# Shared weight tiles for a k pair and more pairs in seven products in a float32 decoder trunk

## The chip, the cores and the metric

The kernel runs on one core of one Trainium2 chip. TensorE does the matrix products, VectorE (DVE in the profile) the elementwise work on two operands, ScalarE (ACT) copies, casts and activation functions, GpSimd (POOL) a few small steps, and SyncE (SP) issues nearly all DMAs. The metric is the time of one execution on the device in microseconds; lower is better. Three runs of the kernel before stand beside one profiled execution.

## The reference

Two pre-norm layers over a stream of 256 positions and 2048 features, all in float32. Layer 0 mixes by sliding-window attention and an mLSTM memory, layer 1 by an attention with forget gates; each is followed by a SwiGLU feed-forward part with 5632 hidden features. The change lies in the feed-forward part and in how weights are loaded:

```python
def swiglu(xn, w_gate, w_up, w_down):
    return (jax.nn.silu(xn @ w_gate) * (xn @ w_up)) @ w_down
...
        h = h + mix.astype(h.dtype)
        h = h + swiglu(rms_norm(h, norm_ffn[layer]), w_gate[layer], w_up[layer], w_down[layer])
    return rms_norm(h, norm_final)
```

## The kernel before

**Three products for one.** A float32 product is made of products on float32r operands. An operand is split in a high part, a rounded copy (ScalarE's cast), and a low part, the difference (VectorE). One product is then three matmuls into the same PSUM bank: high by high, high by low, low by high (`three`, L365 to L368, and the same in `gemm`, L187 to L189). Each is 128x128 weights against 128 x 512 columns. The activations (xh, xl, mh, ml) are split once; the weights come from memory, two k tiles of 512 columns at a time (`load_raw`, tile raw, `CK = 2`), and are split by `split_chunk` into hi (L159, ScalarE) and lo (L160, VectorE). There are six buffers each of hi and lo, four of raw.

**Groups of the feed-forward part.** The 256 positions are two tiles t of 128. `pair_group` (from L373) computes the products of both t with two blocks of 512 columns, `mats`: the same columns of w_gate and w_up, or two neighbouring blocks of w_down. These four results have four PSUM banks (`plain`). It walks over pairs of k tiles in the order of a table of (kind, pair): `ORDER` for gate and up (8 pairs), `DOWN` for the down product (6 or 8 pairs).

- Kind 0, a plain pair: for both matrices a load, a split, and 4 products of three matmuls; 24 matmuls.
- Kind 1, a mixed pair: the 2x2 blocks (two positions tiles, two k tiles, two matrices) are multiplied in seven products, not eight; 21 matmuls. It needs sums of activations (sx, sd; made once by `sums_of`, L222 on) and sums of weight tiles: four VectorE operations of 512 columns into t4 (L404 to L407), split into ht (L261) and lt (L262), two tiles of two k tiles each, besides hi and lo of the first matrix and of one k tile of the second. Four of the seven products go into four further banks (`prods`), which are added up into c when the group's last mixed pair is done (L430 to L434).

The banks swap: the plain banks of a group are the prods banks of the next. Before the change 3 of 8 pairs are mixed in gate/up, 1 of 6 or 2 of 8 in down.

**Order of the groups.** The 11 gate/up groups of a layer are cut in parts (`PARTS`: groups 0 to 2, 3 to 6, 7 to 10). After each part come two down groups over its hidden features; in the last part of layer 1 the second is replaced by two plain `gemm` runs, with `skew` k tiles at their end sorted by t, so that the first t finishes early. After a gate/up group, silu and the product with up are formed on ScalarE and VectorE, and the result is transposed by DMA; the rest of this (`join`) is put into the next group, once its sixth position (or fifth) is reached: copies, a split into mh and ml, and the sums for mixed pairs.

**Who orders the work.** Each engine runs its queue strictly in order. The order in a queue is set when the program is built: a scheduler goes through the operations of all engines by a planned time, so TensorE's matmuls need not stand in the order of the code. A tile of a pool is given out again when all work on the tile that had the buffer is done.

## Time and profile before

| | |
|---|---|
| runs | 2135.94 us median of 3 (2135.59 to 2136.3) |
| profiled execution | span 2134.3 us |
| TensorE | 2118.0 us busy, 9772 matmuls |
| VectorE | 1665.9 us busy, 2116 instructions |
| ScalarE | 1235.5 us busy, 1564 instructions |
| DMA | 418.84 MB, mean 196 GB/s |
| granted clock | 0.998 of full speed |

The feed-forward part of layer 0 lies at about 350 to 1000 us, that of layer 1 at about 1430 to 2134 us; before them are the projections and attention of their layers. In the rows of the trace a line starts with the time from the span's start and the duration, in microseconds; L366 is line 366 of the kernel, and `acc<-lo,xh` says that a matmul writes the tile acc from lo and xh. Groups of rows have a count (x198) and a mean in ns. `<-ACT ht L261` behind a row names what ended an idle time. A matmul row lasts 0.39 us, but the next one starts after 0.23 us, since they are pipelined.

### The profile page before, as it was taken

Reading aid. Unit: us, or ns where it says so; the run is one execution under the profiler, and the core shown is the slowest. Engines: PE = TensorE matmul, PEld = TensorE weight load, DVE = VectorE, ACT = ScalarE, POOL = GpSimd, SP = SyncE. Lnnn points to the kernel's source line nnn. Section 1 sums busy time; section 2 is a strip of 40 time slices with the busy share of each in tenths; the row PEclk is TensorE's granted clock in tenths of the full one; section 3 lists DMA queues with packets and bytes.
Section 4 is the critical chain, followed back from the end, with each engine's and each line's share of the span. In section 5 each row is a group of like instructions: output and inputs, shape, how many; then the busy total and the mean of one; then the engine's idle time right before and its main releaser. Section 6 shows DMA issues by size and latency. Waiting matters only on the chain.

```text
span 2134.3 us, 26801 instructions
## 1 busy us (share of the span) xinstructions
PE 2118.0 (99%) x9772; PEld 1758.6 (82%) x9772; DVE 1665.9 (78%) x2116; ACT 1235.5 (58%) x1564; POOL 40.4 (2%) x61
## 2 busy tenths in 40 slices
PE   8999999999999999999999999999999999999998
PEld 7888888888888888888888888888888888888886
DVE  6665567998899988998745554768998998889984
ACT  6565455665567646666645544556754667556753
POOL 2010000000000000000010000000000000000000
PEclk9999999999999999999999999999999999999999
DMA  8444556666667666776575564655756666656753
GB/s 268 149 151 145 174 183 206 214 210 194 200 205 223 212 206 193 236 210 191 152 236 168 168 178 141 234 185 174 246 187 215 207 207 199 234 188 207 227 198 128
DMA packets 257060, 418.84 MB, mean 196 GB/s; under 512 B 56256, under 2 KB 64544, under 8 KB 256672
## 3 DMA queue, kind: packets, MB, share of 16 engines
q1 hardware_dynamic: 256256, 413.40, 61.1%
q0 software_dynamic: 624, 3.72, 0.5%
q8 instruction: 76, 1.25, 0.2%
q14 instruction: 56, 0.46, 0.1%
q10 hardware_dynamic: 48, 0.02, 0.0%
HBM read 404.48 MB, written 2.11 MB: 191 GB/s over the span
## 4 chain that ended last, share of the span: by engine, by line
PE 98%; ACT 1%; issue 0%; DMA 0%; DVE 0%; POOLq 0%; POOL 0%; DVEq 0%; ACTq 0%
PE acc L367 17%; PE acc L368 17%; PE acc L366 17%; PE acc L187 10%; PE acc L188 10%; PE acc L189 10%; PE prod L368 4%; PE prod L367 4%; PE prod L366 4%; PE pt L239 1%; PE p L290 1%; PE ptm L273 1%; PE po L341 1%; PE pp L333 0%; PE p L283 0%
## 5 line engine op out<-in xcount | busy, mean ns | idle before, releaser
L159 ACT CAST hi<-raw 128x1024 fp32r<-128x1024 f32 (+1 forms) x692 | 705.7, 1033 | 681.2 <-PE acc L368 308.4
L160 DVE TENSOR_TENSOR lo<-raw,hi 128x1024 fp32r<-128x1024 f32 (+1 forms) x692 | 820.4, 1198 | 317.9 <-ACT hi L159 316.3
L367 PE MATMUL acc<-lo,xh 128*128 128x512 f32 x946 | 368.1, 389 | 0.0
L368 PE MATMUL acc<-hi,xl 128*128 128x512 f32 x946 | 366.8, 389 | 0.0
L366 PE MATMUL acc<-hi,xh 128*128 128x512 f32 x946 | 366.4, 389 | 0.0
L187 PE MATMUL acc<-hi,xh 128*128 128x512 f32 (+3 forms) x736 | 276.6, 377 | 0.8 <-ACT hi L159 0.8
L189 PE MATMUL acc<-hi,xl 128*128 128x512 f32 (+3 forms) x736 | 276.6, 376 | 0.0
L188 PE MATMUL acc<-lo,xh 128*128 128x512 f32 (+3 forms) x736 | 276.3, 375 | 0.0
L368 PEld LDWEIGHTS acc<-hi,xl 128*128 128x128 f32 x946 | 177.6, 188 | 36.8
L367 PEld LDWEIGHTS acc<-lo,xh 128*128 128x128 f32 x946 | 177.6, 188 | 36.8
L366 PEld LDWEIGHTS acc<-hi,xh 128*128 128x128 f32 x946 | 177.6, 188 | 36.8
L262 DVE TENSOR_TENSOR lt<-t,ht 128x1024 fp32r<-128x1024 f32 x168 | 199.6, 1216 | 3.6 <-ACT ht L261 3.6
L367 PE MATMUL acc<-lo,mh 128*128 128x512 f32 x514 | 200.3, 390 | 0.0
L366 PE MATMUL acc<-hi,mh 128*128 128x512 f32 x514 | 200.1, 389 | 0.0
L368 PE MATMUL acc<-hi,ml 128*128 128x512 f32 x514 | 198.6, 389 | 0.0
L261 ACT CAST ht<-t 128x1024 fp32r<-128x1024 f32 x168 | 175.0, 1053 | 23.2 <-PE acc L368 13.1
L187 PEld LDWEIGHTS acc<-hi,xh 128*128 128x128 f32 x736 | 138.8, 189 | 24.9 <-ACT hi L159 1.2
L189 PEld LDWEIGHTS acc<-hi,xl 128*128 128x128 f32 x736 | 139.1, 189 | 24.3 <-issue 0.8
L188 PEld LDWEIGHTS acc<-lo,xh 128*128 128x128 f32 x736 | 139.1, 189 | 24.1 <-issue 0.7
L187 PE MATMUL acc<-hi,mh 128*128 128x512 f32 x320 | 125.8, 393 | 1.2 <-ACT mh L261 1.2
L188 PE MATMUL acc<-lo,mh 128*128 128x512 f32 x320 | 125.7, 393 | 0.0
L189 PE MATMUL acc<-hi,ml 128*128 128x512 f32 x320 | 124.0, 390 | 0.0
(306 smaller groups left out, 2768.4 us busy)
## 6 DMA issues: line engine op xcount, KB each, us to landing
raw<-in_w_gate_dram SPq DMA_DIRECT2D x176, 512.0 KB, 4.1
raw<-in_w_up_dram SPq DMA_DIRECT2D x176, 512.0 KB, 4.5
raw<-in_w_down_dram SPq DMA_DIRECT2D x176, 512.0 KB, 4.6
raw<-in_w_in_odd_dram SPq DMA_DIRECT2D x88, 512.0 KB, 3.8
raw<-in_w_in_even_dram SPq DMA_DIRECT2D x64, 512.0 KB, 3.8
raw<-in_w_out_even_dram SPq DMA_DIRECT2D x32, 512.0 KB, 3.5
raw<-in_w_out_odd_dram SPq DMA_DIRECT2D x32, 512.0 KB, 3.9
raw<-in_w_in_odd_dram SPq DMA_DIRECT2D x8, 272.0 KB, 2.9
```

The lines of the kernel that those rows point to most:

```text
L159: latest[0] = nc.scalar.copy(hi[:, :, 0:n], raw[:, :, 0:n])
L160: nc.vector.tensor_tensor(out=lo[:, :, 0:n], in0=raw[:, :, 0:n], in1=hi[:, :, 0:n].bitcast(F32), op=ALU.subtract)
L187: nc.tensor.matmul(o, ah[:, ts], hi, start=(k == 0), stop=False)
L188: nc.tensor.matmul(o, ah[:, ts], lo, start=False, stop=False)
L189: nc.tensor.matmul(o, al[:, ts], hi, start=False, stop=(k == k_all - 1))
L239: nc.tensor.transpose(pt[:, i, t, :], h[:, t, k * P : (k + 1) * P], ident)
L261: nc.scalar.copy(dst_h, src)
L262: nc.vector.tensor_tensor(out=dst_l, in0=src, in1=dst_h.bitcast(F32), op=ALU.subtract)
L273: nc.tensor.transpose(pt[:, i, :], s_, ident)
L366: nc.tensor.matmul(o, ah, hi, start=start, stop=False)
L367: nc.tensor.matmul(o, ah, lo, start=False, stop=False)
L368: nc.tensor.matmul(o, al, hi, start=False, stop=stop)
```

## The change

A weight tile raw now holds four k tiles of 512 columns (`CK = 4`), and there are three of them, shared by everything; hi and lo are as wide, with three buffers each. In the projections and `gemm` a chunk is four k tiles, loaded by two DMAs as large as before. In `pair_group` one raw tile holds a k pair of both matrices (`load_pair`): the second matrix in blocks 0 and 1, the first in 2 and 3. A plain pair is then split by one cast and one difference of 2048 columns. In a mixed pair one split covers three blocks; the four sums are formed by one operation of 1024 columns (its first operand repeated) into td, and two of 512 columns written back into raw; ht and lt are one tile each of four blocks, with one buffer, filled by two splits. Products that need no sums go to TensorE in another order, and the third sum of the activations changes its sign.

The tables have one more mixed pair in the even gate/up groups (positions 1, 3, 5, 6), and in every down group (2 of 6, 3 of 8). The odd gate/up groups keep three, at positions 2, 4 and 6. In the down groups the four adds into h become one, and the last `gemm` sorts its last eight k tiles, not six.

```diff
-CK = 2
+CK = 4
+PK = 2
...
-ORDER = ((0, 0), (0, 1), (1, 2), (0, 4), (1, 3), (0, 5), (1, 6), (0, 7))
+ORDER = (
+    ((0, 0), (1, 1), (0, 2), (1, 3), (0, 4), (1, 5), (1, 6), (0, 7)),
+    ((0, 0), (0, 2), (1, 1), (0, 4), (1, 3), (0, 5), (1, 6), (0, 7)),
+)
 DOWN = {
-    6: ((0, 0), (0, 1), (1, 2), (0, 3), (0, 4), (0, 5)),
-    8: ((0, 0), (0, 1), (0, 3), (1, 2), (0, 4), (1, 5), (0, 6), (0, 7)),
+    6: ((0, 0), (0, 1), (1, 2), (0, 3), (1, 4), (0, 5)),
+    8: ((0, 0), (1, 1), (0, 2), (1, 3), (0, 4), (1, 5), (0, 6), (0, 7)),
 }
...
-    wp = ctx.enter_context(tc.tile_pool(name="wp", bufs=6))
-    wr = ctx.enter_context(tc.tile_pool(name="wr", bufs=4))
+    wp = ctx.enter_context(tc.tile_pool(name="wp", bufs=3))
+    wr = ctx.enter_context(tc.tile_pool(name="wr", bufs=3))
...
+    def load_pair(mats, k0):
+        raw = wr.tile([P, CK, NB], F32, tag="raw", name="raw")
+        for half, (w, c0) in zip((PK, 0), mats):
+            fetch(raw[:, half : half + PK, :], w, k0, c0, NB)
         return raw
...
-        if n < 3:
+        if n < 2:
             ahead.append(load_raw(wi, n * CK, OFF_KS, NB))
...
-            ra, rb = (load_raw(w, k0, c0, NB, fp) for w, c0 in mats)
-            hg, lg = split_chunk(ra, NB)
+            raw = load_pair(mats, k0)
+            hg, lg = split_chunk(raw[:, 1:4, :], NB)
             run_due(todo, pos)
-            t4 = fp.tile([P, 4, NB], F32, tag="t4", name="t4", bufs=1)
-            nc.vector.tensor_tensor(out=t4[:, 0, :], in0=rb[:, 0, :], in1=ra[:, 0, :], op=ALU.subtract)
-            nc.vector.tensor_tensor(out=t4[:, 1, :], in0=rb[:, 1, :], in1=rb[:, 0, :], op=ALU.subtract)
-            nc.vector.tensor_tensor(out=t4[:, 2, :], in0=rb[:, 1, :], in1=t4[:, 0, :], op=ALU.subtract)
-            nc.vector.tensor_tensor(out=t4[:, 3, :], in0=ra[:, 1, :], in1=t4[:, 2, :], op=ALU.subtract)
-            hu = wp.tile([P, CK, NB], F32R, tag="hi", name="hi")
-            lu = wp.tile([P, CK, NB], F32R, tag="lo", name="lo")
-            split_plain(hu[:, 1, :], lu[:, 1, :], rb[:, 1, :])
-            ht, lt = [], []
-            for i in range(2):
-                hs = fp.tile([P, 2, NB], F32R, tag="ht", name="ht")
-                ls = fp.tile([P, 2, NB], F32R, tag="lt", name="lt")
-                split_plain(hs, ls, t4[:, 2 * i : 2 * i + 2, :])
...
+            td = fp.tile([P, 2, NB], F32, tag="td", name="td", bufs=1)
+            nc.vector.tensor_tensor(
+                out=td, in0=raw[:, 0:1, :].broadcast_to([P, 2, NB]), in1=raw[:, 1:3, :], op=ALU.subtract
+            )
+            nc.vector.tensor_tensor(out=raw[:, 0, :], in0=raw[:, 1, :], in1=td[:, 1, :], op=ALU.subtract)
+            nc.vector.tensor_tensor(out=raw[:, 1, :], in0=raw[:, 3, :], in1=raw[:, 0, :], op=ALU.subtract)
+            ht = fp.tile([P, 4, NB], F32R, tag="ht", name="ht", bufs=1)
+            lt = fp.tile([P, 4, NB], F32R, tag="lt", name="lt", bufs=1)
+            split_plain(ht[:, 0:2, :], lt[:, 0:2, :], td)
+            split_plain(ht[:, 2:4, :], lt[:, 2:4, :], raw[:, 0:2, :])
             sh, sl = sums(pair)
...
+            three(plain[0][0], xb[:, t0], lb[:, t0], hg[:, 2, :], lg[:, 2, :], False, False)
+            three(plain[1][0], sh[:, 3, :], sl[:, 3, :], hg[:, 0, :], lg[:, 0, :], False, False)
+            three(prods[0], xa[:, t0], la[:, t0], hg[:, 1, :], lg[:, 1, :], first, last)
+            three(prods[1], sh[:, 0, :], sl[:, 0, :], ht[:, 1, :], lt[:, 1, :], first, last)
+            three(prods[2], sh[:, 2, :], sl[:, 2, :], ht[:, 0, :], lt[:, 0, :], first, last)
+            three(prods[3], sh[:, 1, :], sl[:, 1, :], ht[:, 2, :], lt[:, 2, :], first, last)
+            three(plain[0][1], xb[:, t1], lb[:, t1], ht[:, 3, :], lt[:, 3, :], False, False)
...
-                        gemm(acc, m_of, wd, n * NB, NB, 0, nk, nk, skew=3 if n == 3 else 1)
+                        gemm(acc, m_of, wd, n * NB, NB, 0, nk, nk, skew=2 if n == 3 else 1)
```

More of the change, by code (lines that the diff above doesn't have):

```diff
@@ L42 @@
 MID_DOWN = 5
-RAWS = 4
 PARTS = (0, 3, 7, 11)
@@ L99, in trunk, with fetch, load_raw @@
     nc.scalar.dma_start(gn[0], norm_mix.rearrange("l (k p) -> (l k) p", p=P))
-    def load_raw(w, k0, c0, n, pool=wr):
-        raw = pool.tile([P, CK, NB], F32, tag="raw", name="raw", bufs=4 if pool is wr else RAWS)
-        nc.sync.dma_start(
-            raw[:, :, 0:n], w[k0 * P : (k0 + CK) * P, c0 : c0 + n].rearrange("(k p) n -> p k n", p=P)
-        )
+    def fetch(raw, w, k0, c0, n):
+        m = raw.shape[1]
+        nc.sync.dma_start(raw[:, :, 0:n], w[k0 * P : (k0 + m) * P, c0 : c0 + n].rearrange("(k p) n -> p k n", p=P))
+    def load_raw(w, k0, c0, n):
+        raw = wr.tile([P, CK, NB], F32, tag="raw", name="raw")
+        for half in range(0, CK, PK):
+            fetch(raw[:, half : half + PK, :], w, k0 + half, c0, n)
+        return raw
+    def load_pair(mats, k0):
+        raw = wr.tile([P, CK, NB], F32, tag="raw", name="raw")
+        for half, (w, c0) in zip((PK, 0), mats):
+            fetch(raw[:, half : half + PK, :], w, k0, c0, NB)
         return raw
@@ L248, in split_scaled @@
             pair = 2 * n + half
-            if extra is not None and pair in mixed_of(ORDER):
+            if extra is not None and pair in mixed_of(ORDER[0]):
                 sh, sl, pool = extra
-                j = mixed_of(ORDER).index(pair)
+                j = mixed_of(ORDER[0]).index(pair)
                 def copies(full):
@@ L440, in sums_x @@
         def sums_x(pair):
-            j = mixed_of(ORDER).index(pair)
+            j = mixed_of(ORDER[0]).index(pair)
             return sx[0][:, j, :, :], sx[1][:, j, :, :]
```

54 lines of the change are left out of this document (22 added, 32 removed).

## The prediction

> **What bounds the kernel now.** I read the page first (busy times, slices, the chain that ended last), then what TensorE waited for, then the FFN by windows, one for each group of matmuls.
>
> ```profile
> span 2134.3 us, 26801 instructions
> PE 2118.0 (99%) x9772; PEld 1758.6 (82%) x9772; DVE 1665.9 (78%) x2116; ACT 1235.5 (58%) x1564; POOL 40.4 (2%) x61
> DVE  6665567998899988998745554768998998889984
> PEclk9999999999999999999999999999999999999999
> PE 98%; ACT 1%; issue 0%; DMA 0%; DVE 0%; POOLq 0%; POOL 0%; DVEq 0%; ACTq 0%
> ```
>
> TensorE is busy for 99% at the full clock, and the chain lies on it for 98%. VectorE is the next: 78% overall, but 8s and 9s in the two FFN stretches. Busy time of pipelined matmuls can hide small gaps, so the waits:
>
> ```profile
> PE pg L144 <- DMA gn<-in_norm_mix_dram: 4.1, 1, 4.1
> PE acc L187 <- ACT mh L261: 1.2, 1, 1.2
> PE pt L239 <- DMA h<-in_x_dram: 1.1, 1, 1.1
> PE acc L187 <- ACT hi L159: 0.8, 1, 0.8
> PE pp L333 <- DVE s L325: 0.2, 1, 0.2
> ```
>
> TensorE waits for almost nothing after the first microseconds. Now the second part of the FFN of layer 0: gate/up groups 3, 4, 5, 6 and two down groups (a window, its length, busy time of each engine).
>
> ```profile
> core 0: us, PE busy (x) PEld busy (x) DVE busy (x) ACT busy (x) POOL busy (x), PEclk, DMA share, GB/s
> 540.40:581.88 41.48, 41.48 (x184) 34.36 (x183) 32.18 (x37) 22.41 (x24) 0.00 (x0) 1.00 0.66 213
> 581.88:623.36 41.48, 41.48 (x184) 34.36 (x183) 38.26 (x46) 27.56 (x30) 0.00 (x0) 1.00 0.68 216
> 623.36:664.84 41.48, 41.48 (x184) 34.36 (x183) 39.25 (x50) 28.41 (x31) 0.00 (x0) 1.00 0.68 216
> 664.84:706.32 41.48, 41.48 (x184) 34.36 (x183) 38.59 (x50) 28.30 (x31) 0.00 (x0) 1.00 0.69 213
> 706.32:748.48 42.16, 42.16 (x187) 34.92 (x186) 37.19 (x45) 26.39 (x28) 0.00 (x0) 1.00 0.63 201
> 748.48:790.64 42.16, 42.16 (x187) 34.92 (x186) 36.43 (x44) 20.41 (x21) 0.00 (x0) 1.00 0.62 201
> ```
>
> A gate/up group has 183 matmuls and 41.48 us: 0.2267 us each, without a gap. VectorE has 2.2 to 3.2 us of room in a group that also joins the one before. So fewer matmuls save their full 0.2267 us as long as VectorE and ScalarE deliver in time, and the room there is some 7%.
>
> **The change, part by part.** *Matmuls removed.* A pair of k tiles costs 24 matmuls plainly and 21 in seven products. One more pair is mixed in six of eleven gate/up groups of each layer (0, 2, 4, 6, 8, 10) and in each of six down groups, in layer 1 five: 23 pairs, 69 matmuls, 69 x 0.2267 = **-15.6 us**.
>
> *VectorE's work.* One instruction after the other takes:
>
> ```profile
> 568.83 0.69 DVE L404 TENSOR_TENSOR t<-raw 128x512 f32<-128x512 f32 x1
> 569.44 0.68 DVE L405 TENSOR_TENSOR t<-raw 128x512 f32<-128x512 f32 x1
> 570.04 0.68 DVE L406 TENSOR_TENSOR t<-raw,t 128x512 f32<-128x512 f32 x1
> 570.64 1.22 DVE L160 TENSOR_TENSOR lo<-raw,hi 128x1024 fp32r<-128x1024 f32 x1
> 571.78 0.68 DVE L407 TENSOR_TENSOR t<-raw,t 128x512 f32<-128x512 f32 x1
> ```
>
> From start to start 0.60 us for 512 columns, 1.14 for 1024; 0.54 for each further 512 makes 1.67 for 1536 and 2.21 for 2048. A mixed pair was 3 x 1.14 (lo, two lt) + 5 x 0.60 = 6.42, and becomes 1.67 + 1.14 (td) + 2 x 0.60 + 2 x 1.14 = 6.29. A plain pair goes from 2.28 to 2.21. An even gate/up group (four mixed, four plain) gains 34.0 - 30.66 = 3.3: the windows' 38.26 and 38.59 become 41.6 and 41.9, or 1.4 more where a join now has sums to form (four 128x128 operations and a split). TensorE needs 180 x 0.2267 = 40.8. An odd group loses 0.7 (39.25 becomes 38.5, of 41.48); a down group gains 3.2 and stays under 41.5. Over these six windows VectorE goes from 221.9 to 235 of 247.5: no bound on the whole, but over TensorE in the even groups, where a lead won before must carry it.
>
> *The ht and lt tiles, the term that decides.* Before, ht and lt were two tiles of two columns blocks, released half by half; now they are one tile of four with one buffer. How such a release goes in the profile:
>
> ```profile
> 564.65 0.39 PE L368 MATMUL prod<-ht,sx 128*128 128x512 f32 x1
> 565.12 1.06 ACT L261 CAST ht<-t 128x1024 fp32r<-128x1024 f32 x1
> 566.01 0.39 PE L368 MATMUL acc<-ht,xl 128*128 128x512 f32 x1
> 566.41 2.39 DVE L262 TENSOR_TENSOR lt<-t,ht 128x1024 fp32r<-128x1024 f32 x2
> 566.49 1.05 ACT L261 CAST ht<-t 128x1024 fp32r<-128x1024 f32 x1 [0.30 <-DVE lo L160]
> 573.72 0.39 PE L366 MATMUL prod<-ht,sx 128*128 128x512 f32 x1
> ```
>
> The second product on ht ends its half at 565.04 and ScalarE refills it at 565.12; the last ends at 566.40, and the other half is refilled at 566.49. These halves are used at 573.72: a plain pair and nine matmuls lie between, and hide the split. I compared the order written for TensorE in the changed kernel. After the last matmul that reads a mixed pair's ht comes, before the first that reads the next pair's: in groups 0, 2, 6 and 10 of both layers, where positions 5 and 6 are both mixed, **one** matmul; in group 8 none; in group 4 fifteen; in group 5 and 9 (positions 2 and 4) and in the first down group of the last part (3 and 5) six; elsewhere nine or more.
>
> From the start s of that last matmul: it ends at s + 0.39, ScalarE starts at s + 0.48 as above, a half is copied by s + 1.53, TensorE starts 0.06 later (the start-up rows below: cast ends 8.19, matmul 8.25), at s + 1.59. The second half follows at ScalarE's spacing, some 0.96 (two casts in 2.00 us in the row 573.31, quoted below), so TensorE can use it at s + 2.55.
>
> ```profile
> 573.31 2.00 ACT L159 CAST hi<-raw 128x1024 fp32r<-128x1024 f32 x2
> 576.68 1.05 ACT L261 CAST ht<-t 128x1024 fp32r<-128x1024 f32 x1 [0.30 <-PE acc L368]
> ```
>
> With one matmul between, the first would have started at s + 0.45: 1.14 lost; the third at s + 2.04 waits for the second half: 0.51 more, 1.65. Eight such: 13.2. Group 8, none between, first half only: 1.59 - 0.23 = 1.36, twice: 2.7. Six between: 0.51, six times: 3.1. Sum **+19.0 us**. Bounds: nothing, if the halves are released singly after all; and 1.2 us more in each of the ten (the 1024 lt after the ht, if VectorE comes to it late, as the next group's lo stands before the lt in its queue in groups 8 and 10), 31. I take 19: each link has its row.
>
> The Trainium skill (Perfetto Trace Analysis, Optimization Strategy) says that a gap which repeats on the engine that should be saturated can mean too few buffers for the next tile. No gap repeats in this trace; by that rule this single buffer would make one, and its sum is the one just made.
>
> *The start of the even groups.* Prods of the old group lie in the banks that the new group's plain products want; VectorE must empty them. In group 6 and 10 VectorE has, from the last lt of the old group to the bank of the third product, sd 0.60, td 1.14, lo 1.67, u 0.60, raw 0.60, lt 1.14 and c 0.60: 6.35. TensorE has 20 matmuls in between, 4.53; counted on in the same way from the release before, VectorE's last lt stands 1 us ahead of its need, so 0.8 is lost, and as much again at the lo of the third pair that stands behind. 1.6 in four groups: **+6.2**. Bounds: none, and 3 us in all ten even groups with a mixed pair second after another group, 30. I take the count.
>
> *Start-up.* The first chunk has now four k tiles:
>
> ```profile
> 7.16 1.03 ACT L159 CAST hi<-raw 128x1024 fp32r<-128x1024 f32 x1
> 8.23 1.22 DVE L160 TENSOR_TENSOR lo<-raw,hi 128x1024 fp32r<-128x1024 f32 x1 [0.45 <-ACT hi L159]
> 8.25 1.22 PE L187 MATMUL acc<-hi,xh 128*128 128x512 f32 x2 [0.83 <-ACT hi L159]
> ```
>
> The cast and the difference double, 2.1 us later at most for both, and another 512 KB must land; transposes now go ahead of the first matmul and win some back. Between 0 and 4, taken **+1.5**. The Trainium skill (Perfetto Trace Analysis, Optimizing Scalar/DVE Operations) speaks against larger operations here: where these engines are not saturated but make others wait, breaking them up can help; by it the loss would be nearer the 4.
>
> *At nothing.* The loads and their time to land:
>
> ```profile
> raw<-in_w_gate_dram SPq DMA_DIRECT2D x176, 512.0 KB, 4.1
> raw<-in_w_down_dram SPq DMA_DIRECT2D x176, 512.0 KB, 4.6
> ```
>
> They stay as many and as large; one pair fewer is in flight, but a pair lasts 4.8 us or more on TensorE, as long as a load takes. Chunks of four in the projections and output: TensorE never waits there now, and two more tiles are ready; without that cover 1 us each. Three adds fewer per down group on VectorE, the new sign in the sums, the longer sorted tail (it frees the first half earlier, the last matmul ends the same): 0, within 0.5. ScalarE copies the same columns; its 28 of 41.5 us leave room, its order matters only in the chain above. POOL and its queue are unchanged.
>
> Sum: -15.6 + 19.0 + 6.2 + 1.5 = +11.1. The span becomes 2145.4; the median of the runs, 2135.94, lies 1.6 above the span, so **2147**.
>
> **The rivals.** *One: the cover holds and the matmuls are saved.* If ht is freed by halves or VectorE and ScalarE keep ahead, only start-up and the odd 0.5 remain: -15.6 + 1.5 + 0 to 3 gives 2122 to 2125. For it: no wait of TensorE in the FFN now, 94.9% of VectorE in the stretch. Against: one matmul of cover against a chain of 1.59 us. It decides below some 0.6 us lost at each of the ten places, together with the group starts.
>
> *Two: VectorE becomes the bound of the even groups.* Then each of eight groups with a join lasts VectorE's 41.9 to 43.0 and the 2.2 us that it idles even now: 44.1 to 45.2 against 41.48, +2.6 to +3.7, 21 to 30 us; the ends of the other groups give back 8, start-up takes 1.5: 2150 to 2160. For it: 8s and 9s in the slices, 95% in group 5. Against: much of the idle is a wait for tiles that TensorE frees, and is filled when VectorE is late.
>
> *Three: gains and waits cancel*, within 4 us of before: what happens if the group starts cost nothing and the chain a little less.
>
> **How the numbers follow.** Forecast (2138 to 2155 by itself) 0.45; rival two, or both mechanisms in full up to 2168, 0.25; rival one 0.22; rival three 0.08. A difference under 0.2% (4.3 us) can't be told from none. So faster 0.22, same 0.08, slower 0.70. The range leaves out the lower half of rival one and the upper end of rival two: 2124 to 2163.
>
> **What would show it.** TensorE's matmuls fall by 69. In even groups except 4 there is a gap of 1.1 us or more before the first product on ht of position 6, its releaser ScalarE's ht copy, with a second of 0.5 behind; even groups last 42 to 44.5 us instead of 40.8, down groups about 41.5. If TensorE's waits for ht stay under 5 us in all, the chain was wrong; if the even groups last long with TensorE waiting for lo and lt, VectorE's total was the cause; if start-up moves by over 4, the chunk size.

## The result and the profile after

The changed kernel takes 2271.65 us (median of four runs, 2269.23 to 2274.98) against 2135.99 before: a ratio of 1.0638, 95% interval 1.0623 to 1.0653. It is slower, as forecast, but by 135.7 us and not by 11: the range ended at 2163. The profiled execution has a span of 2267.5 us in a run of 2269.23.

The page of the changed kernel, its busy times, VectorE's slices and the chain that ended last:

```profile
span 2267.5 us, 25185 instructions
PE 2165.9 (96%) x9703; PEld 1753.1 (77%) x9703; DVE 1727.9 (76%) x1766; ACT 1215.0 (54%) x1234; POOL 39.0 (2%) x61
...
DVE  5565567988889898889645555578888988789885
...
PE 45%; DVE 21%; DMA 17%; ACT 8%; issue 5%; SPq 2%; ACTq 0%; DVEq 0%; POOLq 0%; POOL 0%
```

The 69 matmuls are gone (9772 to 9703). VectorE is busy for 62 us more with 350 instructions fewer, about as counted (13 us more in six of the 33 groups that `pair_group` walks); ScalarE is busy for 20 us less. TensorE's busy time grew by 48 us with fewer matmuls, so its 96% do not measure its gaps. What stands out is the chain. It lay on TensorE for 98% and now does for 45%; DMA, which had nothing of it, has 17%, VectorE 21%. TensorE waits for an engine that itself waits, at the far end for a load.

Where it waits is seen one step further up, in what ScalarE waited for (us in all, times, longest). After:

```profile
ACT hi L172 <- DMA raw<-in_w_up_dram: 211.4, 93, 8.6
ACT hi L172 <- DMA raw<-in_w_down_dram: 100.2, 33, 6.0
```

and before, the same two places:

```profile
ACT hi L159 <- DMA raw<-in_w_gate_dram: 14.6, 9, 1.6
ACT hi L159 <- DMA raw<-in_w_down_dram: 13.9, 10, 5.7
```

ScalarE's cast of fresh weights now waits 312 us for loads, eleven times as long. Of the waits that TensorE itself has on record, 91.6 us in all, 41.2 are for these casts, 14.3 for lo and 8.8 for ht. That is less than what was lost; the rest lies inside TensorE's busy time.

By windows, for groups of layer 0 (a window from the first matmul of a group to the next group's; its length, busy time of each engine, clock):

```profile
core 0: us, PE busy (x) PEld busy (x) DVE busy (x) ACT busy (x) POOL busy (x), PEclk, DMA share, GB/s
353.05:400.94 47.89, 44.53 (x191) 35.42 (x190) 37.57 (x45) 26.99 (x32) 0.69 (x1) 0.96 0.46 155
442.71:492.90 50.19, 44.64 (x182) 34.43 (x180) 43.95 (x44) 29.69 (x25) 0.00 (x0) 0.97 0.57 187
747.80:791.99 44.19, 42.08 (x185) 34.20 (x183) 37.57 (x36) 26.95 (x23) 0.00 (x0) 1.00 0.62 199
836.15:877.63 41.48, 41.48 (x184) 34.37 (x183) 36.68 (x31) 19.32 (x15) 0.00 (x0) 1.00 0.57 185
```

Groups 0 and 2 last 47.9 and 50.2 us where their 180 matmuls take 40.8; a down group 44.2 where it should take 41.5; group 7, behind two down groups, runs without a gap. In group 0 VectorE has only 37.6 us of work: it cannot be the whole cause.

One gap read through the engines, at the end of group 10 of layer 0 (rows of ScalarE, SyncE's queue, VectorE and TensorE):

```profile
985.32 1.49 ACT L172 CAST hi<-raw 128x1536 fp32r<-128x1536 f32 x1 [1.07 <-DMA raw<-in_w_up_dram]
...
988.45 5.96 SPq L495 DMA_TRANSPOSE turned<-c  x4
994.51 0.53 SPq L106 DMA_DIRECT2D raw<-in_w_gate_dram  x1
...
999.22 0.69 DVE L421 TENSOR_TENSOR raw<-raw 128x512 f32<-128x512 f32 x1
1005.12 1.22 DVE L275 TENSOR_TENSOR lt<-raw,ht 128x1024 fp32r<-128x1024 f32 x1
...
1004.09 0.88 SPq L106 DMA_DIRECT2D raw<-in_w_down_dram  x2
1009.55 1.90 ACT L172 CAST hi<-raw 128x2048 fp32r<-128x2048 f32 x1 [5.85 <-DMA raw<-in_w_down_dram]
1011.36 1.04 ACT L274 CAST ht<-td 128x1024 fp32r<-128x1024 f32 x1
1011.50 0.50 PE L379 MATMUL acc<-hi,mh 128*128 128x512 f32 x1 [2.78 <-ACT hi L172]
1012.45 0.73 PE L379 MATMUL prod<-ht,sx 128*128 128x512 f32 x2 [0.45 <-ACT ht L274]
...
1014.42 0.63 PE L380 MATMUL acc<-lo,mh 128*128 128x512 f32 x1
1014.85 0.63 PE L381 MATMUL acc<-hi,ml 128*128 128x512 f32 x1
```

The mixed pair that is cast at 985.32 has its last sum at 999.22, but that sum lies in the load tile itself, and the lt made from it ends at 1006.34: the tile is held for 21 us from its cast, 26.6 from the issue of its load at 979.78, and the last 6.4 of them, from the end of the sum at 999.91, for the lt alone. Only three tiles exist. So the next group's first load is not issued before 1004.09, when another tile is freed, and lands at 1009.5; ScalarE stands 5.85 us, with the ht copies of the last mixed pair, whose data are there, behind the waiting cast; and TensorE stops for both. Ahead of the pair of loads at 994.51 four transposes hold SyncE's queue for 5.96 us.

A gap costs more than its own length here. The matmuls at 1014.42 and 1014.85 start 0.43 us apart, not 0.23, and the granted clock is 0.88 from 1003.90 to 1018.50. Over the whole span it is 0.985, which lacks 0.015 x 2267.5 = 34 us of full speed, against 4 before (0.998): by this estimate up to 30 of the 135.7 us are slow matmuls behind gaps.

### The profile page after: what moved, and what is told of

Read it like the earlier page. It is cut to its first block, busy times and chain, and to the rows that moved or that the text cites. A ratio compares the mean times of both kernels' runs of the same rounds, so it can differ in the third digit from the quotient of the medians.

```text
span 2267.5 us, 25185 instructions
## 1 busy us (share of the span) xinstructions
PE 2165.9 (96%) x9703; PEld 1753.1 (77%) x9703; DVE 1727.9 (76%) x1766; ACT 1215.0 (54%) x1234; POOL 39.0 (2%) x61
## 4 chain that ended last, share of the span: by engine, by line
PE 45%; DVE 21%; DMA 17%; ACT 8%; issue 5%; SPq 2%; ACTq 0%; DVEq 0%; POOLq 0%; POOL 0%
DMA raw<-in_w_up_dram 11%; PE acc L202 10%; PE acc L201 10%; PE acc L200 10%; DVE lo L173 10%; DMA raw<-in_w_down_dram 5%; ACT hi L172 5%; PE acc L380 3%; DVE lt L275 3%; PE acc L381 3%; PE acc L379 3%; DVE td L417 2%; ACT ht L274 1%; SPq L495 1%; SPq L106 1%
## 5 line engine op out<-in xcount | busy, mean ns | idle before, releaser
L173 DVE TENSOR_TENSOR lo<-raw,hi 128x2048 fp32r<-128x2048 f32 (+4 forms) x388 | 814.4, 2101 | 342.8 <-ACT hi L172 341.9
L172 ACT CAST hi<-raw 128x2048 fp32r<-128x2048 f32 (+4 forms) x388 | 680.7, 1757 | 691.7 <-PE acc L202 221.4
L379 PE MATMUL acc<-hi,mh 128*128 128x512 f32 x437 | 165.2, 402 | 27.3 <-ACT hi L172 19.4
L380 PE MATMUL acc<-lo,mh 128*128 128x512 f32 x437 | 175.1, 401 | 6.9 <-DVE lo L173 6.9
L381 PE MATMUL acc<-hi,ml 128*128 128x512 f32 x437 | 171.8, 398 | 0.8 <-DVE ml L275 0.8
L274 ACT CAST ht<-td 128x1024 fp32r<-128x1024 f32 x107 | 112.1, 1048 | 97.8 <-PE acc L381 67.8
L275 DVE TENSOR_TENSOR lt<-td,ht 128x1024 fp32r<-128x1024 f32 x107 | 130.6, 1220 | 31.3 <-ACT ht L274 31.3
L417 DVE TENSOR_TENSOR td<-raw 128x1024 f32<-128x1024 f32 x107 | 130.6, 1221 | 13.2 <-DMA raw<-in_w_up_dram 6.8
L274 ACT CAST ht<-raw 128x1024 fp32r<-128x1024 f32 x107 | 112.0, 1046 | 36.9 <-DVE raw L421 36.6
L275 DVE TENSOR_TENSOR lt<-raw,ht 128x1024 fp32r<-128x1024 f32 x107 | 130.5, 1220 | 0.8 <-ACT ht L274 0.7
```

The lines of the kernel that those rows point to most:

```text
L172: latest[0] = nc.scalar.copy(hi[:, 0:m, 0:n], raw[:, :, 0:n])
L173: nc.vector.tensor_tensor(out=lo[:, 0:m, 0:n], in0=raw[:, :, 0:n], in1=hi[:, 0:m, 0:n].bitcast(F32), op=ALU.subtract)
L274: nc.scalar.copy(dst_h, src)
L275: nc.vector.tensor_tensor(out=dst_l, in0=src, in1=dst_h.bitcast(F32), op=ALU.subtract)
L379: nc.tensor.matmul(o, ah, hi, start=start, stop=False)
L380: nc.tensor.matmul(o, ah, lo, start=False, stop=False)
```

## The experiments

Times are medians in us; each kernel was compared with the kernel before on the same chip (2135.64 to 2136.16). *Own sums* is one and the same edit in several kernels: all four sums lie in td, now of four blocks, and none goes back into raw:

```diff
-            td = fp.tile([P, 2, NB], F32, tag="td", name="td", bufs=1)
+            td = fp.tile([P, 4, NB], F32, tag="td", name="td", bufs=1)
...
-            nc.vector.tensor_tensor(out=raw[:, 0, :], in0=raw[:, 1, :], in1=td[:, 1, :], op=ALU.subtract)
-            nc.vector.tensor_tensor(out=raw[:, 1, :], in0=raw[:, 3, :], in1=raw[:, 0, :], op=ALU.subtract)
+            nc.vector.tensor_tensor(out=td[:, 2, :], in0=raw[:, 1, :], in1=td[:, 1, :], op=ALU.subtract)
+            nc.vector.tensor_tensor(out=td[:, 3, :], in0=raw[:, 3, :], in1=td[:, 2, :], op=ALU.subtract)
...
-            split_plain(ht[:, 2:4, :], lt[:, 2:4, :], raw[:, 0:2, :])
+            split_plain(ht[:, 2:4, :], lt[:, 2:4, :], td[:, 2:4, :])
```

| kernel | time | ratio, 95% interval |
|---|---|---|
| changed kernel | 2271.65 | 1.0638 (1.0623 to 1.0653) |
| old tables | 2187.85 | 1.0242 (1.0227 to 1.0257) |
| own sums | 2197.13 | 1.0285 (1.0268 to 1.0302) |
| ht and lt in halves | 2243.80 | 1.0508 (1.0492 to 1.0524) |
| three of eight in all gate/up groups | 2228.42 | 1.0433 (1.0417 to 1.0448) |
| old tables, own sums | 2139.47 | 1.0018 (1.0009 to 1.0027) |
| old tables, a fourth load tile | 2161.31 | 1.0119 (1.0105 to 1.0133) |
| old tables, transposes from ScalarE | 2226.19 | 1.0423 (1.0409 to 1.0437) |
| own sums, halves | 2208.85 | 1.0342 (1.0327 to 1.0356) |
| own sums, three of eight, new down | 2161.80 | 1.0120 (1.0105 to 1.0136) |
| own sums, four of eight, old down | 2186.39 | 1.0235 (1.0221 to 1.0249) |
| the same, two sums left out | 2137.89 | 1.0010 (1.0000 to 1.0019) |
| the same, sums on GpSimd | 2228.54 | 1.0435 (1.0418 to 1.0452) |
| own sums, four of eight in 4 and 8 only | 2144.70 | 1.0041 (1.0027 to 1.0055) |
| own sums, four of eight in 2, 6, 10 only | 2156.38 | 1.0096 (1.0081 to 1.0111) |
| before, 2 of 6 in down | 2133.23 | 0.9989 (0.9980 to 0.9998) |
| before, new down | 2129.60 | 0.9970 (0.9958 to 0.9981) |
| before, all new tables | 2308.21 | 1.0804 (1.0787 to 1.0820) |
| before, all new tables, sums on GpSimd | 2350.11 | 1.1001 (1.0984 to 1.1017) |

### Layout or tables

The first set undoes one part of the change at a time. Old tables in the new layout:

```diff
-ORDER = (
-    ((0, 0), (1, 1), (0, 2), (1, 3), (0, 4), (1, 5), (1, 6), (0, 7)),
-    ((0, 0), (0, 2), (1, 1), (0, 4), (1, 3), (0, 5), (1, 6), (0, 7)),
-)
+ORDER = (((0, 0), (0, 1), (1, 2), (0, 4), (1, 3), (0, 5), (1, 6), (0, 7)),) * 2
...
-    6: ((0, 0), (0, 1), (1, 2), (0, 3), (1, 4), (0, 5)),
-    8: ((0, 0), (1, 1), (0, 2), (1, 3), (0, 4), (1, 5), (0, 6), (0, 7)),
+    6: ((0, 0), (0, 1), (1, 2), (0, 3), (0, 4), (0, 5)),
+    8: ((0, 0), (0, 1), (0, 3), (1, 2), (0, 4), (1, 5), (0, 6), (0, 7)),
```

> The changed kernel with the old tables: 3 of 8, 1 of 6 and 2 of 8 mixed, no two mixed pairs side by side; tiles and buffers as changed. A (a mixed pair keeps its raw tile until its last lt, so loads are issued late): fewer pairs hold tiles, 2155 to 2180. B (the single ht and lt tile): a plain pair now always lies between, 2145 to 2155. C (the two mixed pairs side by side, and their number): what is lost comes back but for the start, 2140 to 2160. D (wide tiles and three buffers by themselves): still over 2220.

Own sums, the edit above:

> The changed kernel, but all four sums of weight tiles go into td (four blocks), none back into raw, so raw is free once the sums and lo are made, not after the last lt. A: loads are issued some 5 us earlier in every mixed pair, the wait of ScalarE for loads (211 us for w_up, 100 for w_down) falls to less than half, 2185 to 2225. B and C: hardly a change, 2250 to 2275. D: 2240 to 2270.

The prediction's main term, ht and lt given back as two tiles each:

```diff
-            ht = fp.tile([P, 4, NB], F32R, tag="ht", name="ht", bufs=1)
-            lt = fp.tile([P, 4, NB], F32R, tag="lt", name="lt", bufs=1)
-            split_plain(ht[:, 0:2, :], lt[:, 0:2, :], td)
-            split_plain(ht[:, 2:4, :], lt[:, 2:4, :], raw[:, 0:2, :])
+            ht, lt = [], []
+            for src in (td, raw[:, 0:2, :]):
+                hs = fp.tile([P, 2, NB], F32R, tag="ht", name="ht")
+                ls = fp.tile([P, 2, NB], F32R, tag="lt", name="lt")
+                split_plain(hs, ls, src)
+                ht += [hs[:, 0, :], hs[:, 1, :]]
+                lt += [ls[:, 0, :], ls[:, 1, :]]
```

> The changed kernel with ht and lt as two tiles of two blocks with two buffers each, as before the change; the same bytes. B: the chain behind a mixed pair is gone, 2190 to 2220 or less. A: raw is still held for the last lt, which comes a little earlier, 2235 to 2265. C and D: 2255 to 2275.

No even group with a fourth mixed pair:

```diff
-                    fp, par, x_of, sums_x, [(w_gate[layer], g * NB), (w_up[layer], g * NB)], ORDER[g % 2], todo
+                    fp, par, x_of, sums_x, [(w_gate[layer], g * NB), (w_up[layer], g * NB)], ORDER[1], todo
```

> The changed kernel with the odd groups' table in all gate/up groups: 3 of 8, positions 2, 4 and 6; down groups with the additional pairs. 18 matmuls a layer more than the changed kernel (8.2 us in all). C: only the even groups' 80 us of lost time go, 2185 to 2205, and the odd groups keep the 26 they lose now. A: the same way, each group then loses what groups 5 and 9 lose now (5 us), 2195 to 2230. B: 2180 to 2200. D: over 2250.

Measured: 2187.85, 2197.13, 2243.80, 2228.42. A, the load tile held too long, has the second and third in its ranges and the fourth at its edge; the old tables came out 8 us above A's range and in no other. The largest single step is own sums, 74.5 us off the changed kernel by one tile of two more blocks; halves take off 27.9. What stands ahead of the loads in SyncE's queue, before and after that edit, shows the path. In the changed kernel (waits of SyncE's queue):

```profile
SPq L106 <- DVE lo L173: 1094.7, 242, 15.1
SPq L106 <- DVE lt L275: 221.2, 86, 11.5
```

and with own sums:

```profile
SPq L106 <- DVE lo L173: 1140.4, 253, 11.0
SPq L106 <- DVE td L421: 240.7, 58, 9.9
```

In the first, 86 loads wait until an lt frees their tile; in the second none does, the last sum frees it. ScalarE's waits for loads fall with it (own sums):

```profile
ACT hi L172 <- DMA raw<-in_w_up_dram: 62.0, 34, 6.6
ACT hi L172 <- DMA raw<-in_w_down_dram: 40.8, 23, 4.1
```

103 us in place of 312. With the old tables and sums in raw, 52 us are lost without any new mixed pair: the layout is a cause by itself.

### Which part of the layout

Old tables with own sums; old tables with a fourth load tile in the feed-forward (sums in raw); old tables with the transposes on ScalarE's queue; and, since the tables were to be tried on the old layout, before with 2 of 6 in down:

```diff
-    def load_pair(mats, k0):
-        raw = wr.tile([P, CK, NB], F32, tag="raw", name="raw")
+    turn = [0]
+
+    def load_pair(mats, k0, fp):
+        pool = fp if turn[0] % 4 == 3 else wr
+        turn[0] += 1
+        raw = pool.tile([P, CK, NB], F32, tag="raw", name="raw", bufs=1 if pool is fp else 3)
```

```diff
-                        nc.sync.dma_start_transpose(turned[b][:, :, t, :], flat[:, b, t, :])
+                        nc.scalar.dma_start_transpose(turned[b][:, :, t, :], flat[:, b, t, :])
```

```diff
-    6: ((0, 0), (0, 1), (1, 2), (0, 3), (0, 4), (0, 5)),
+    6: ((0, 0), (0, 1), (1, 2), (0, 3), (1, 4), (0, 5)),
```

> The changed tiles with the old tables (2187.85 in the first series), and the four sums in td, so that raw is free before the last lt. H (what is left, 52 us over before, is raw held by the second lt): 2140 to 2155. N (three pair tiles are too few in flight, whoever holds them) and Q (loads stand behind the transposes in SyncE's queue, 6 us for each join): 2170 to 2185.

> The changed tiles with the old tables, and a fourth weight tile in the feed-forward part (every fourth pair loads into it); sums in raw as changed. N: the waits for loads (130 and 79 us of ScalarE) nearly go, 2140 to 2155. H: a held tile matters less but the pair behind still waits, 2155 to 2175. Q: a load is issued one pair earlier, so the 6 us of transposes are covered, 2140 to 2160.

> The changed tiles with the old tables, and the DMA transposes issued from ScalarE's queue, not from SyncE's, so that no load stands behind them. Q: the groups with a join lose nothing more, 2145 to 2165, if ScalarE has room for the 5 us of issue per group (27 of 41.5 busy). H and N: 2180 to 2200.

> The kernel before with one table of the change alone: 2 of 6 pairs mixed in down (positions 2 and 4), all tiles as before. Four groups save 3 matmuls each, 12 x 0.2267 = 2.7 us. If matmuls saved count in full where VectorE has room (28.8 and 29.6 of 32 busy, 4.1 more): 2133.0 to 2134. If VectorE binds in these groups (33 and 33.7 against 31.3): 2136 to 2145.

Measured: 2139.47, 2161.31, 2226.19, 2133.23. The first is 0.5 us below H's range, the second in it; the third is outside all its ranges; in the fourth the saved matmuls count in full, as expected. Own sums alone bring the new layout within 3.8 us of before, 48.4 off; a fourth tile, with the long hold left in, takes off 26.5. Both the hold and the number of tiles count. With own sums and the old tables the windows are at the length of their matmuls (groups 2 and 6 of layer 0 and the down group behind):

```profile
437.16:478.64 41.48, 41.48 (x184) 34.35 (x183) 38.82 (x39) 27.14 (x23) 0.00 (x0) 1.00 0.65 213
667.95:709.43 41.48, 41.48 (x184) 34.35 (x183) 38.48 (x39) 26.08 (x22) 0.00 (x0) 1.00 0.66 210
709.43:751.59 42.16, 42.16 (x187) 34.91 (x186) 35.51 (x33) 25.09 (x20) 0.00 (x0) 1.00 0.70 228
```

The single ht tile, the three load tiles and the wider operations cost nothing there, with a plain pair between any two mixed ones. This kernel still waits 75.1 us for w_up on ScalarE; TensorE does not feel it. A wait is a loss only where it reaches the engine that sets the end.

The transposes' run cost 38 us and settles nothing: on ScalarE's queue they stand among the casts. What the loads behind the transposes on SyncE's queue cost in all remains open; one such place is read below.

### The tables, with own sums

> Sums in td (2197.13 in the first series) and ht and lt in two tiles of two blocks each with two buffers. B (what is left over the matmuls is the single ht tile, above all between the two mixed pairs side by side): the groups 2, 6 and 10 lose 6 to 7 us now and would lose 2 or less, 2150 to 2170. V (VectorE's total, 43.6 to 44.0 us busy in these groups against 40.8 of matmuls): hardly better, 2185 to 2200.

> Sums in td, the odd table in all gate/up groups (3 of 8), the additional pairs in down alone. B and V alike: the gate/up groups run as in the kernel with the old tables (41.48 us each); 11 pairs more in down save 7.5 us against its 2139.47 if the down groups keep up: 2131 to 2134. If the first down group of a part loses as it does now (5 and 2 us): 2140 to 2150.

> Sums in td, 4 of 8 in the even gate/up groups, the old table in down. 12 pairs save 8.2 us. The even groups lose as in the second series (48 us in all), down groups nothing: 2170 to 2185. If the loss of the even groups came from work pushed into them by down: 2140 to 2160.

> The kernel before with the new tables in down (2 of 6, 3 of 8), and three load tiles for mixed pairs, not four, since the sums of activations take their place. 11 pairs, 33 matmuls, 7.5 us: 2128 to 2129.5 if all counts. If three load tiles starve the mixed pairs as the shared tiles did: 2140 to 2170.

The edits are combinations of those shown: halves with own sums; three of eight everywhere with the new down table; the new gate/up table with the old down table. The last puts the new down table in the kernel before, with RAWS = 3 in place of 4 to make room. (Beside the four raw tiles of plain pairs, the kernel before has RAWS = 4 more for mixed pairs, each for a k pair of one matrix: two plain and two mixed k pairs of both matrices fit in them, three of either kind in the changed kernel.) Measured: 2208.85, 2161.80, 2186.39, 2129.60. The first two came out above both of their ranges, the third 1.4 us above the first of its ranges, the last within 0.1 us of its first.

Halves with own sums are 11.7 us slower than own sums alone. So the 27.9 that halves gave the changed kernel are hardly the chain through ht that the prediction argued: TensorE's waits for ht are 11.7 us there, not fewer than the changed kernel's 8.8. A shorter hold of the load tile, as its lt can be made earlier, is possible, but SyncE's waits for an lt fall only from 221.2 to 194.1 us. What the halves save stays open.

The new gate/up table costs 46.9 us on the 2139.47. Its windows, groups 0, 1 and 2 of layer 0, then 4 and 6:

```profile
352.06:395.79 43.73, 43.01 (x196) 35.03 (x194) 37.02 (x44) 26.62 (x31) 0.69 (x1) 1.00 0.53 176
395.79:437.31 41.52, 41.52 (x184) 34.34 (x183) 37.28 (x36) 27.88 (x24) 0.00 (x0) 1.00 0.65 207
437.31:485.98 48.67, 43.98 (x181) 32.84 (x180) 43.62 (x44) 28.86 (x25) 0.00 (x0) 1.00 0.58 189
...
594.57:635.37 40.80, 40.80 (x181) 33.79 (x180) 33.87 (x30) 26.16 (x22) 0.00 (x0) 1.00 0.58 188
679.58:725.85 46.27, 43.10 (x182) 33.10 (x181) 43.63 (x44) 29.42 (x25) 0.00 (x0) 1.00 0.63 199
```

Group 4, behind a group without a join, lasts its matmuls' 40.80. Groups 2 and 6 have 43.6 us of work for VectorE in a place of 40.8: rival two of the prediction, with 5.1 and 2.6 us of VectorE's idle time on top. In group 2 that idle time is again a load (ScalarE and SyncE's queue):

```profile
464.99 1.48 ACT L172 CAST hi<-raw 128x1536 fp32r<-128x1536 f32 x1 [6.66 <-DMA raw<-in_w_up_dram]
...
454.13 5.13 SPq L495 DMA_TRANSPOSE turned<-c  x4
459.37 0.52 SPq L106 DMA_DIRECT2D raw<-in_w_gate_dram  x1
459.93 0.47 SPq L106 DMA_DIRECT2D raw<-in_w_up_dram  x1
```

The load behind four transposes lands as the cast has waited 6.66 us. Two tiles come free just after the transposes began, when a lo of VectorE ends at 455.22 and a last sum at 456.55; whichever of them it takes, its load is issued 2.8 to 4.2 us later than it could be.

The new down table costs 22.3 us with wide tiles (2161.80 against 2139.47; its gate/up groups also have the changed kernel's order of three of eight) and wins 6.5 with the old ones, nearly its 33 x 0.2267 = 7.5. Of the 22.3, 4.9 are one wait of TensorE at the layer change, for VectorE's add into h, which the kernel of 2139.47 does not have. In the kernel with the old tiles, the fastest of all, VectorE is busier than in any of the windows shown of before and TensorE has no gap (the down group behind group 6 of layer 0):

```profile
704.17:745.65 41.48, 41.48 (x185) 34.36 (x183) 40.26 (x49) 28.00 (x31) 0.00 (x0) 1.00 0.71 217
```

So neither VectorE at 97% nor three load tiles for mixed pairs stop it there. The runs don't show which property of the wide tiles does.

### VectorE's share

From the kernel with the new gate/up table (2186.39), two of a mixed pair's three sum operations are left out, or all three go to GpSimd; and the new tables are tried on the old layout, where memory leaves two load tiles for mixed pairs, one for each matrix (RAWS = 2 in place of 4), once more with its sums on GpSimd:

```diff
-            nc.vector.tensor_tensor(out=td[:, 2, :], in0=raw[:, 1, :], in1=td[:, 1, :], op=ALU.subtract)
-            nc.vector.tensor_tensor(out=td[:, 3, :], in0=raw[:, 3, :], in1=td[:, 2, :], op=ALU.subtract)
...
-            split_plain(ht[:, 2:4, :], lt[:, 2:4, :], td[:, 2:4, :])
+            split_plain(ht[:, 2:4, :], lt[:, 2:4, :], td[:, 0:2, :])
```

```diff
...
-            nc.vector.tensor_tensor(out=td[:, 2, :], in0=raw[:, 1, :], in1=td[:, 1, :], op=ALU.subtract)
+            nc.gpsimd.tensor_tensor(out=td[:, 2, :], in0=raw[:, 1, :], in1=td[:, 1, :], op=ALU.subtract)
...
```

> The wide tiles with sums in td, 4 of 8 in even gate/up groups, the old table in down (2186.39), and two of the three sums of weight tiles left out in each mixed pair (the second split repeats the first sums): part of the computation is left out, 1.2 us of VectorE per mixed pair, 4.8 in an even group. V (VectorE's total): groups 2, 6 and 10 fall from 46.3 to 48.7 to 41 to 43, all in all 2140 to 2155. If order or buffers hold them: 2175 to 2187.

> The kernel before with all the new tables (4 of 8 in even groups, 2 of 6, 3 of 8), on the old half-wide tiles, two load tiles for mixed pairs, not four, to make room for the sums of activations. 69 matmuls fewer, 15.6 us. V: the even groups have 43 us of VectorE to 40.8 of matmuls there too and the pairs 5 and 6 side by side, 2140 to 2175. If the wide tiles were the whole cause: 2120 to 2124.

> The wide tiles with sums in td, 4 of 8 in even gate/up groups, the old table in down (2186.39), and the sums of weight tiles formed by GpSimd, which is idle. V: 2.3 us of VectorE per mixed pair go away, 2128 to 2150, if GpSimd makes 2048 columns in under 10 us. If GpSimd and VectorE slow each other, or the longer way of the sums decides: 2180 to 2260.

> All the new tables on the old tiles as in e14, and the sums of weight tiles formed by GpSimd. V and no contention: 2120 to 2126, all matmuls saved count. If GpSimd's way is too long: over e14.

Without the two operations: 2137.89, 48.5 us less, better than the theory asked. Groups 2 and 6 of layer 0 are then near their 40.8:

```profile
437.54:478.51 40.97, 40.97 (x182) 33.66 (x180) 38.06 (x37) 27.50 (x23) 0.00 (x0) 1.00 0.76 243
667.15:708.70 41.55, 41.10 (x182) 33.72 (x181) 38.23 (x36) 28.43 (x25) 0.00 (x0) 1.00 0.71 227
```

The loads, transposes, ht tiles and matmuls are as many as before; what has shrunk is VectorE's work, and with it the time until a load tile is free. So in these groups the rest hangs on VectorE's work per mixed pair, a late load included: in group 2 the load that stood behind the transposes now goes out at 450.72, before they start at 452.46. How much is VectorE's time and how much the tile freed sooner, the run does not part.

With the sums on GpSimd it gets worse, 2228.54, as the second of its ranges has it (operations of GpSimd, whose spans are rough, then of VectorE; count, busy us, mean ns, idle time before):

```profile
L417 POOL TENSOR_TENSOR td<-raw 128x1024 f32<-128x1024 f32 x96 | 287.4, 2994 | 1044.8 <-DVE lo L173 358.9 <-DVE lt L275 270.4 <-DMA raw<-in_w_up_dram 215.0
L421 POOL TENSOR_TENSOR td<-raw,td 128x512 f32<-128x512 f32 x96 | 240.1, 2501 | 7.5
...
L173 DVE TENSOR_TENSOR lo<-raw,hi 128x2048 fp32r<-128x2048 f32 (+4 forms) x388 | 952.5, 2466 | 366.6 <-ACT hi L172 365.3
```

and the same row with the sums on VectorE:

```profile
L173 DVE TENSOR_TENSOR lo<-raw,hi 128x2048 fp32r<-128x2048 f32 (+4 forms) x388 | 820.5, 2118 | 314.7 <-ACT hi L172 311.0 <-PE acc L381 2.5
```

A subtraction of 512 columns has a span of 2.2 to 2.5 us there against 0.68 on VectorE, and VectorE's own lo went from 2118 to 2466 ns: 132 us more in that one row. The Trainium skill (Perfetto Trace Analysis, Optimizing Scalar/DVE Operations) says that the two engines share a read port, so that such a move may not help. The trace agrees with that: lo of 1536 columns, in mixed pairs, went from 1752 to 2315 ns, and lo of 1024 columns, outside the feed-forward part, stayed at 1222. That the port is the reason is not shown apart.

The new tables on the old layout came out at 2308.21, far over both of its ranges, and at 2350.11, over that, as the second part of its expectation has it. With loads for one mixed pair at a time, its casts starve (ScalarE's waits at the cast of a mixed pair's second matrix, kernel without GpSimd; 1.7 us before):

```profile
ACT hi L264 <- DMA raw<-in_w_up_dram: 69.6, 33, 5.6
```

So they are no test of the tables: too few load tiles are in them as a second cause.

### A fourth pair, or a fourth pair in the wrong group

Two last kernels split the even groups, with nothing left out:

```diff
-                    fp, par, x_of, sums_x, [(w_gate[layer], g * NB), (w_up[layer], g * NB)], ORDER[g % 2], todo
+                    fp, par, x_of, sums_x, [(w_gate[layer], g * NB), (w_up[layer], g * NB)], ORDER[0 if g in (4, 8) else 1], todo
```

```diff
-                    fp, par, x_of, sums_x, [(w_gate[layer], g * NB), (w_up[layer], g * NB)], ORDER[g % 2], todo
+                    fp, par, x_of, sums_x, [(w_gate[layer], g * NB), (w_up[layer], g * NB)], ORDER[0 if g in (2, 6, 10) else 1], todo
```

> Sums in td, old tables for down, four of eight only in groups 4 and 8 of both layers, three of eight (the changed order) in all other gate/up groups. In the kernel with four of eight in all even groups (2186.39) groups 4 and 8 lasted their matmuls' 40.80 us, with VectorE busy for 34; groups 2, 6 and 10, which also form a group's join, lasted 46 to 49 with VectorE busy for 43.5. Theory that the even groups lose because a fourth mixed pair and a join together exceed VectorE's time: the fourth pair is free in 4 and 8, four groups save 0.68 us each on the 2139.47 of the old tables: 2136 to 2141 (the upper end if groups 5 and 9 behind them miss the lead). Rival that the fourth pair costs by itself (the order of positions, the single ht): a third of the 47 us lost with all even groups: 2150 to 2158.

> The complement: sums in td, old tables for down, four of eight only in groups 2, 6 and 10. Theory of VectorE's total: nearly all of the loss stays. Over their matmuls groups 2, 6 and 10 lost 7.9, 5.5 and 5.5 us in layer 0 (7.4, 5.0, 5.5 in layer 1) and the down groups behind group 2 3.2 and 3.9: 2139.47 - 6 x 0.68 + 37 + 7 gives 2179, 2165 to 2182 with what groups 4 and 8 no longer take. Rival that the fourth pair costs by itself: half or more of the groups, 2160 to 2165.

Measured: 2144.70, between the two theories, and 2156.38, below both. Over the 2139.47 they cost 5.2 and 16.9 us; with group 0 as well, all together cost 46.9. One thing in the first expectation is not so: groups 4 and 8 do form a join, that of groups 3 and 7 (in the kernel of 2186.39 VectorE makes its ml at 622.75, inside group 4's window). What sets them apart is that the group before them, the first of its part, has none. In the first kernel, group 4 is free and group 5 behind it pays:

```profile
584.66:625.46 40.80, 40.80 (x181) 33.78 (x180) 34.86 (x31) 26.28 (x22) 0.00 (x0) 1.00 0.58 188
625.46:668.44 42.98, 42.38 (x185) 34.11 (x183) 39.37 (x40) 27.00 (x23) 0.00 (x0) 1.00 0.64 203
```

In the second, group 2 has the same four mixed pairs and the same join as in the rows above, and group 0, two groups ahead of it, three mixed pairs in place of four; so has group 4 ahead of group 6 (groups 0, 1, 2, then 6):

```profile
352.65:395.21 42.56, 42.56 (x194) 35.22 (x193) 36.29 (x44) 26.05 (x32) 0.69 (x1) 1.00 0.57 198
395.21:436.69 41.48, 41.48 (x185) 34.35 (x183) 36.20 (x34) 27.34 (x23) 0.00 (x0) 1.00 0.65 192
436.69:479.42 42.73, 41.80 (x182) 33.46 (x180) 41.74 (x43) 28.43 (x24) 0.00 (x0) 1.00 0.67 210
...
671.04:713.71 42.67, 41.94 (x182) 33.47 (x180) 40.99 (x42) 28.53 (x24) 0.00 (x0) 1.00 0.67 207
```

42.73 us against 48.67 in group 2, and 42.67 against 46.27 in group 6: no group carries its own price. Over groups 0 to 2 VectorE is busy for 114.2 us here (36.29 + 36.20 + 41.74) beside 546 matmuls of 0.2267, 123.8 us, and the groups last 126.8; with group 0 at four of eight for 117.9 (37.02 + 37.28 + 43.62) beside 543 matmuls, 123.1 us, and they last 133.9. VectorE's totals are under the matmuls' time in both: what runs out is the lead. A group may ask for more of VectorE than it gives only as far as finished tiles stand ready from the groups before, and three buffers of hi and lo hold two pairs beside the one in use. That the same group lasts longer behind another predecessor is shown; that finished tiles are what carries this is argued from it. One more thing goes with it: with the late VectorE, the load in group 2 falls behind the transposes, as read above, and here it goes out at 452.30, just before they start at 453.23. How much a buffer is worth, and how much the place in SyncE's queue, was not measured.

## Why the prediction was right and wrong

The direction held, the size did not. The account, from kernels that differ by one part: new layout with own sums +3.5 us, new tables on it +57.7 (with the matmuls saved), sums written back into raw +74.5; together 135.7. The shares depend on the order in which the parts are taken: with the sums in raw first, the layout costs 51.9 and the new tables on it 83.8.

**Matmuls removed, -15.6.** Right in count, and only there: 9772 to 9703. In the kernel before with the new down table such matmuls pay 6.5 of 7.5.

**"At nothing": "one pair fewer is in flight, but a pair lasts 4.8 us or more on TensorE, as long as a load takes".** This is the step that failed, by 74.5 us with the new tables and 48.4 with the old. It counted how long a load takes and how long TensorE needs for a pair, and not how long a tile is held between. The diff showed it: the second and third sum go into raw, the lt made from them is the last reader, and that lt waits for the one ht tile. The hold was 26.6 us from the issue of the load in the place read above. Old tables with and without this, 2187.85 and 2139.47, show it without any other part of the change. The sentence on ScalarE in the same paragraph, "its order matters only in the chain above", failed with it: a cast that waits for a load keeps ht copies behind it whose data are ready.

**The ht and lt tiles, +19.0, "the term that decides".** Not borne out. The chain of releases exists, but TensorE's waits for ht are small (changed kernel):

```profile
PE prod L379 <- ACT ht L274: 8.8, 25, 1.2
```

25 waits of 0.35 us in the mean, not ten of 1.1 and ten of 0.5; and with own sums two half tiles make the kernel 11.7 us slower. In the changed kernel itself halves save 27.9, for a reason that stays open. The Trainium skill's rule on repeated gaps and too few buffers (Perfetto Trace Analysis, Optimization Strategy) came true for the load tiles, where a fourth saves 26.5 us with the old tables, and not, as far as the runs show, for ht.

**The start of the even groups, +6.2, and rival two, 21 to 30.** (1.6 in four groups is 6.4; the 0.2 changes nothing.) The mechanism was right in part in rival two, and the size too small in both. VectorE's time in groups with a join was put at 41.9 to 43.0 and measured 43.5 to 44.2; with the idle time the group was to last 44.1 to 45.2, and groups 2 and 10 lasted 50 in the changed kernel, groups 2, 6 and 10 46 to 49 with own sums. But rival two gave every group with a join the same price, and group 4, which has one, lasted its 40.80 with own sums. With own sums the new gate/up table loses 46.9 + 12 x 3 x 0.2267 = 55 us over its matmuls, and 48.5 of them go when VectorE has 1.2 us less in each mixed pair and frees the load tile that much sooner. "A lead won before must carry it" stood in the text, without a number for the lead.

**Start-up, +1.5 within 0 to 4.** Right in range: the feed-forward part starts at 353.05 us against 350.09, 3.0 later. The place was another. TensorE's row in the changed kernel:

```profile
11.31 1.97 PE L252 MATMUL pt<-ident,h 128*128 128x128 f32 x8 [4.07 <-DMA h<-in_x_dram]
```

It waits for the second part of the stream, whose load stands in SyncE's queue behind two loads of weights, where there was one; the doubled cast, the prediction's reason, is hidden behind that.

**Down groups "about 41.5".** The one shown of the changed kernel lasted 44.2 (747.80 above), the one on the old tiles 41.48 (704.17 above): there the table does what it should.

**What would make it wrong.** The prediction's test "if TensorE's waits for ht stay under 5 us in all, the chain was wrong" came out at 8.8 and so would have kept a false term: the waits were there, as the end of another queue. A test on the loads was missing.

## What to carry to other kernels

Before sharing or shrinking load tiles, count from the program how long one is held, from the issue of its load to its last reader, and divide by the number of tiles; an intermediate result written back into a load tile lengthens that by its own wait. A tile of its own for two sums was worth 74 us with the new tables and 48 with the old, and the kernel before had one. An engine that is over its time in some groups and under it in others is no average: it lives on a lead won before, and here a fourth mixed pair in one group was paid for two groups later. The same table of products that lost 22 us in one layout won 6.5 in the other, and this is the version to keep: the kernel before with 2 of 6 and 3 of 8 in down, 2129.60 us, a ratio of 0.9970 (0.9958 to 0.9981).

## What was not expected of the hardware

Four transposes by DMA hold the queue that issues them for 5.1 to 6.0 us (454.13 and 988.45 above), 1.3 to 1.5 each, and loads behind them are not issued before: tiles free at 455.22 and 456.55 had their loads issued from 459.37 on.

With GpSimd's subtractions in the kernel, VectorE's lo of 1536 columns took 2315 ns in the mean, not 1752.

The granted clock is 0.96 and 0.97 in the two windows of the changed kernel shown above that have the longest gaps; behind a gap of 2.78 us the matmuls start 0.43 us apart for some 2 us, and over the span the clock is 0.985 against 0.998 before. The slowest kernel of all has 0.974. It is not the time lost alone that counts: group 2 with own sums lasted 48.67 us at a clock of 1.00, where no single wait of TensorE is over 1.6 us.
